# Low parts of weights by an accumulating DMA instead of a VectorE subtraction, in a two-layer hybrid decoder

## The chip, the cores and the metric

The kernel runs on one core of a Trainium2 chip. The time is device microseconds (us) of one execution of the whole program, from start to end; a run of the kernel before took 1132.09 us (median of three runs, 1131.34 to 1132.42). Engines are named as in the profile: PE is TensorE's matrix multiplication and PEld its weight load, DVE is VectorE, ACT is ScalarE, POOL is GpSimd, SP is SyncE, which issues the transfers. Transfers run on 16 DMA engines that all queues share.

## What is computed

Two decoder layers on 512 prompt tokens and 8 x 8 sample tokens (576 rows, D_MODEL 1024), all in float32:

```python
h = rmsnorm(x, g_norm)
z = h @ w_in                      # 1024 x 5700: rq rk rv rz aq ak av az iq ik iw gr ga
o_r, s_new = retention(rq, rk, rv, s0)
u_r = (group_norm(o_r) * silu(rz)) @ w_o_ret
o_a = sparse_attention(aq, ak, av, top-k by the indexer iq, iw, ik)
u_a = (o_a * silu(az)) @ w_o_att
x = x + (sigmoid(gr) * u_r + sigmoid(ga) * u_a) @ w_out
x = x + sigmoid(x @ w_ple_gate) * (p @ w_ple_proj)
```

Nearly all of the arithmetic is products of the 576 rows with weights. The outputs are the rows after two layers and the new keys, values and retention states.

## The kernel before, in words

**Two-part products.** A float32 factor is split into a high part, rounded to the type float32r (`fp32r` in the profile), and a low part, the factor minus its high part. A product is then three matmuls into one PSUM bank: high times high, high times low of the one factor, low times high of the other. In `proj_a` (lines 457 to 477) the weight is the stationary operand (`pm<-xh,whi`, `pm<-xl,whi`, `pm<-xh,wlo` in the profile, 288 columns each); in `proj_b` (479 to 497) and `proj_kx` (499 to 522) the rows are stationary and the weight moves (`pm<-whi,xh`, `pm<-whi,xl`, `pm<-wlo,xh`, 256 to 320 columns). In each, the low part of a weight is wanted first by the third matmul.

**Weights.** All weights of both layers are one sequence of 148 pieces, at most 128 x 1024 elements (512 KB); this text counts them from 0. `PLAN` sets the order. In layer 0: pieces 0 to 4 are kx (keys and values), 5 to 7 iq (the indexer's queries), 8 and 9 rv0, 10 and 11 rv1 (retention values), 12 to 15 az, 16 and 17 aq0, 18 and 19 aq1 (attention queries), then 12 pieces for retention heads, then gates and outputs: gr, ga, wo, wout, pp, wpg. Layer 1 repeats this from piece 74 (iq 79 to 81, rv0 82 and 83, rv1 84 and 85, aq1 92 and 93).

`load_weights` issues each load from SP into one of two staging buffers (`wst`, 128 x 1024). `convert` takes one of three buffers `whi` and one of three `wlo`, has ACT round the staged piece into `whi`, has DVE subtract into `wlo`, and then gives the staging buffer back. `drop`, or the end of `proj_b` and `proj_kx`, gives `whi` and `wlo` back when PE has used the piece. So at any time PE uses one or two pieces, and the rest of the three are ready or in preparation. In `proj_b` both pieces of a weight are used for each of five row tiles, so the second piece of the next weight finds a free buffer only at the end of the fifth tile.

**Side work.** Beside the projections run streams for the indexer's top-k, attention, retention and norms. Their matmuls stand between the projections' in PE's queue. Reciprocal square roots are one `pow` on POOL each, with DVE before and after it.

**Order.** `Streams` (from line 195) writes out each engine's instructions by list scheduling: of all streams' next instructions it takes the one that a model of the engines could start first. The engines then run their queues in that order and wait on semaphores. `_duration` and the DMA rule in `go` are that model's prices.

Of the kernel before, what the change touches and what calls it, by code (L numbers as in the profile page):

```python
# [11 lines left out]
FT = mybir.dt.float32  # L12
# [3 lines left out]
AF = mybir.ActivationFunctionType  # L16
OP = mybir.AluOpType
# [101 lines left out]
def _val(x):  # L119
    return x() if callable(x) else x  # L120
# [14 lines left out]
def _free(ap):  # L135
    n = 1
    for s, c in list(ap.ap)[1:]:
        n *= c
    return n


def _duration(eng, name, out, aps, a, k):
    n = max(_free(x) for x in aps)
    psum = any(x.space == PSUM for x in aps[1:])
    if eng == "PE":
        if name == "transpose":
            return 0.110
        lhs = aps[1]
        if lhs.dtype == FT:
            if _free(lhs) <= 32:  # L150
                return 0.030 + n * 0.4e-3
            return 4 * max(n, 64) / 2.4e3 * (0.55 if _free(lhs) <= 64 else 1.0)
        return max(n, 64) / 2.4e3 + 0.003
    if eng == "DVE":
        if name == "memset":
            return (n + 8) / 0.96e3
        ptr = sum(1 for x in aps[1:] if _free(x) == 1 and n > 4 and x.space != PSUM)
        if name in ("tensor_scalar", "tensor_copy") and not psum and all(x.dtype == FT for x in aps[:2]):
            return (n / 2 + 66) / 0.96e3 + 0.062 * min(ptr, 2)
        return (n + 64) / 0.96e3 + 0.062 * min(ptr, 2)  # L160
    if eng == "ACT":
        ptr = sum(1 for x in aps[1:] if _free(x) == 1 and n > 1)
        return (n + (61 if psum else 112)) / 1.2e3 + 0.093 * min(ptr, 2)
    if eng == "POOL":
        return 0.3 + 0.165 * n
    return {"page": 0.5, "gather": 0.74}.get(name, 0.47)

# [25 lines left out]


class Streams:
    """Emits the instructions of many sequential streams in the order in which a model of the engines could
    start them, so that each engine's program order follows what is ready."""

    HOP = {("DVE", "DVE"): 0.13, ("ACT", "ACT"): 0.13, ("POOL", "POOL"): 0.1, ("PE", "PE"): 0.0, ("SP", "SP"): 0.0,
           ("ACT", "PE"): 0.23, ("DVE", "PE"): 0.21, ("PE", "DVE"): 0.2, ("PE", "ACT"): 0.2, ("POOL", "DVE"): 0.07,  # L200
# [76 lines left out]
    def go(self):  # L277
        clock = self.clock
        while True:
            while self.run:  # L280
                st, value = self.run.pop(0)
                self._advance(st, value)
            if not self.heads:
                return
            best = None
            for i, st in enumerate(self.heads):
                key = (max(clock[st[3].eng], st[4]), st[1], st[2])
                if best is None or key < best[0]:
                    best = (key, i)
            st = self.heads.pop(best[1])  # L290
            op = st[3]
            start = best[0][0]
            op.fn(*op.a, **op.k)  # L293
            end = start + op.dur
            clock[op.eng] = end
            if op.eng == "SP" and op.name != "page":
                size = _val((op.a[0] if op.a else op.k["out"]).nbytes)
                self.dma = max(self.dma, start + 1.1) + size / 0.35e6
                end = self.dma + 1.0
            self._note(op, end)  # L300
            self._advance(st, None)
# [3 lines left out]
def tile_hybrid_decoder(ctx: ExitStack, tc: tile.TileContext, A, O):  # L305
    nc = tc.nc
    ctx.enter_context(tc.manual_schedule())
    K = Streams()
    V, S, PE, SP, G = (Engine(n, o) for n, o in (("DVE", nc.vector), ("ACT", nc.scalar), ("PE", nc.tensor),
                                                 ("SP", nc.sync), ("POOL", nc.gpsimd)))  # L310
# [7 lines left out]
    def slots(pool, name, shape, dtype, n):  # L318
        return Slots([pool.tile(shape, dtype, name=f"{name}{i}") for i in range(n)])
# [35 lines left out]
    WST = slots(cp, "wst", [128, 1024], FT, 2)  # L355
# [33 lines left out]
    ready, paged = Event(), Event()  # L389
    second, third = Event(), Event()  # L390

    # ---- weights: one ordered sequence of units, each split into two float32r parts as it lands
    W = {}

    class Unit:
# [32 lines left out]
    stage_ev = {}  # L428

    def load_weights(units):  # L430
        for n, (u, src, size) in enumerate(units):
            if n == 1:
                yield second
            if n == 3:
                K.set(third)
            t = yield Get(WST)
            yield SP.dma_start(t[:, :size], src)
            K.spawn(convert(u, t, size, stage_ev[n], stage_ev[n + 1]), PRIO["convert"])

    def convert(u, t, size, prev, done):  # L440
        yield prev
        hi = yield Get(WHI)
        lo = yield Get(WLO)
        yield S.activation(hi[:, :size], t[:, :size], AF.Copy)
        yield V.tensor_tensor(lo[:, :size], t[:, :size], hi[:, :size].bitcast(FT), OP.subtract)
        K.put(WST, t)
        K.set(u.evs[len(u.parts)])
        u.parts.append((hi, lo))
        K.set(u.ev)
        K.set(done)  # L450
# [106 lines left out]
    def layer(l, xh, xl, kxb):  # L557
# [3 lines left out]
        def side(gen, prio, *events):  # L561
            ev = Event()

            def wrap():
                yield from gen
                for e in events:
                    K.set(e)
                K.set(ev)

            sides.append(ev)  # L570
            K.spawn(wrap(), prio)
# [45 lines left out]
        def stats():  # L617
            yield V.memset(ssq[:, T:], 1.0)
            ps = yield Get(BANK["tr"])
            for j in range(5):  # L620
                yield PE.matmul(ps[:, j:j + 1], ssq[:, j * 128:(j + 1) * 128], ones, start=True, stop=True)
            yield from rsqrt(rcol[:, :5], ps[:, :5], 1.0 / D, EPS)
            K.put(BANK["tr"], ps)
            K.set(e_r)
            yield ready
            ps = yield Get(BANK["tr"])
            for j in range(4):
                yield PE.transpose(ps[:, j * 128:(j + 1) * 128], bc(rcol[:, j:j + 1], [128, 128]), ident)
            yield S.activation(R[:, :NP], ps, AF.Copy)
            K.put(BANK["tr"], ps)  # L630
            ps = yield Get(BANK["tr"])
            yield PE.transpose(ps[:, :128], bc(rcol[:, 4:5], [128, 128]), ident)
            yield S.activation(R[:, NP:], ps[:, :NS], AF.Copy)
            K.put(BANK["tr"], ps)
            K.set(e_rq)
# [262 lines left out]
        def head(j, u, g, kv, oT, done):  # L898
            L = max(256, (j + 1) * 128)
            bias = con("cb") if j == 0 else scs[j]  # L900
            q = qst[j, u][:, (g % 2) * 2 + kv]
            P = yield Get(T2)
            b = yield Get(BANK["tq"])
            ps = b[:, :L]
            yield PE.matmul(ps, q, kdh[:, 1 + kv, :L], start=True, stop=False)
            yield PE.matmul(ps, q, kdl[:, 1 + kv, :L], start=False, stop=True)
            yield from softmax(ps, bias, P[:, :L], b)
            PT = yield Get(T2)
            pT = yield Get(BANK["ta"])
            W_ = (j + 1) * 128  # L910
            for k in range(j + 1):
                yield PE.transpose(pT[:, k * 128:(k + 1) * 128], P[:, k * 128:(k + 1) * 128], ident)
            K.put(T2, P)
            yield S.activation(PT[:, :W_], pT[:, :W_], AF.Copy)
            K.put(BANK["ta"], pT)
            for k in range(j + 1):
                yield PE.matmul(oT[kv * 64:(kv + 1) * 64, g * 128:(g + 1) * 128], av[:, k, kv * 64:(kv + 1) * 64],
                                PT[:, k * 128:(k + 1) * 128], start=k == 0, stop=k == j)
            K.put(T2, PT)
            K.put(HD, None)  # L920
            K.set(done)

        HD = Slots([None] * HEADS_IN_FLIGHT)

        def attend():
            yield e_k
            for j in range(4):
# [4 lines left out]
                for u in range(2):  # L932
                    yield e_q[j, u]
                    for g in (2 * u, 2 * u + 1):
                        for kv in range(2):
                            yield Get(HD)
                            K.spawn(head(j, u, g, kv, oT, done), PRIO["attend"])
                yield done
# [256 lines left out]
        side(stats(), 0)  # L1195
        side(tables(), PRIO["tables"])
        for j in range(1, 4):
            side(indexer(j), PRIO["indexer"], e_sc[j])
        side(indexer_s(), PRIO["indexer_s"], e_sc[4])
        side(attend(), PRIO["attend"])  # L1200
        side(attend_s(), PRIO["attend_s"])
# [262 lines left out]

PLAN = _plan("kx iq rv0 rv1 az0 az1 az2 az3 aq0 aq1 rt0 rt1 rt2 rt3")
HEADS_IN_FLIGHT = 3
PRIO = dict(convert=0, load=1, tables=6, indexer=7, indexer_s=3, attend=3, attend_s=5, ret_p=6, ret_s=4)
NSLOT = dict(s4=3, qs=5, t2=5, hi=3, lo=3)

# [81 lines left out]
```

## Time and profile before

| | |
|---|---|
| runs | 1132.09 us median (1131.34 to 1132.42) |
| span of the profiled execution | 1130.3 us, 1.8 us under the median of the runs |
| instructions in the profile | 21562, of them 8586 on PE |
| share of the span in which each is busy | PE 99%, PEld 94%, DVE 64%, ACT 45%, POOL 4% |
| transfers | 105.92 MB, mean 94 GB/s; 93.61 MB read from HBM |
| granted TensorE clock | full in all 40 slices of the span |

The profile is one execution. Busy PE is modelled and says that matmuls follow each other without a gap that can be seen, not that each is at its shortest. What the transfers move by source: 96 loads of `in_wa`, 16 of `in_wb`, 16 of `in_wo` with 512 KB each are the bulk of the weights. No transfer is issued from POOL.

### The profile page before, as it was taken

The numbers are of one execution on the slowest core, as the hardware profiler recorded it, in microseconds if no ns is written. First come the engines' busy times: TensorE is split into PE (matmuls) and PEld (weight loads), VectorE is DVE, ScalarE is ACT, GpSimd is POOL, SyncE is SP. The second block draws the span as 40 slices with busy tenths as digits, with TensorE's granted clock in tenths as the row PEclk, the third lists the DMA queues.
The fourth block names the chain that finished last, engine by engine and source line by source line (L and its number), as shares of the span: only waits on it lengthen the run. The fifth ranks groups of instructions, "written<-read, shape, count | busy, mean of one in ns | idle before, by whom it ended". The sixth has DMA issues, their size and how long they took to land.

```text
span 1130.3 us, 21562 instructions
## 1 busy us (share of the span) xinstructions
PE 1116.5 (99%) x8586; PEld 1058.9 (94%) x8586; DVE 725.6 (64%) x1883; ACT 512.5 (45%) x1084; POOL 45.7 (4%) x52
## 2 busy tenths in 40 slices
PE   8999999999999999999999999999999999999998
PEld 7899988888899999999999999888889999999998
DVE  6799988876464444543658999888654553544343
ACT  6643566647443232324546336656563422222331
POOL 0100200000000000000010012000000000000000
PEclk9999999999999999999999999999999999999999
DMA  6442221322122222523336112222212222234231
GB/s 196 139 133 76 76 75 52 102 78 78 59 75 75 93 76 92 172 92 109 100 118 181 59 57 94 74 79 80 73 60 78 75 78 91 75 130 144 93 113 48
DMA packets 43895, 105.92 MB, mean 94 GB/s; under 512 B 6418, under 2 KB 18578, under 8 KB 43794
## 3 DMA queue, kind: packets, MB, share of 16 engines
q1 hardware_dynamic: 43794, 104.55, 27.4%
q8 instruction: 67, 1.10, 0.4%
q14 instruction: 34, 0.28, 0.1%
HBM read 93.61 MB, written 10.91 MB: 92 GB/s over the span
## 4 chain that ended last, share of the span: by engine, by line
PE 91%; DVE 4%; DMA 2%; ACT 2%; issue 1%; SPq 0%; POOL 0%; DVEq 0%; ACTq 0%; POOLq 0%
PE pm L293 72%; PE oT L293 5%; PE tq L293 4%; PE acc L293 3%; PE tr L293 3%; PE ta L293 3%; DVE wlo L293 1%; DMA wst<-in_wb 1%; ACT whi L293 1%; DVE misc L293 1%; DMA x<-in_xT 1%; DVE silz L293 0%; DMA wst<-in_wq 0%; DVE qs L293 0%; DVE ol L293 0%
## 5 line engine op out<-in xcount | busy, mean ns | idle before, releaser
L293 PE MATMUL pm<-xl,whi 128*128 128x288 f32 x1536 | 458.7, 299 | 0.0
L293 PE MATMUL pm<-xh,wlo 128*128 128x288 f32 x1536 | 458.4, 298 | 0.0
L293 PE MATMUL pm<-xh,whi 128*128 128x288 f32 x1536 | 458.0, 298 | 0.4 <-DVE misc L293 0.4
L293 PEld LDWEIGHTS pm<-xl,whi 128*128 128x128 f32 x1536 | 290.1, 189 | 3.2 <-issue 2.4
L293 PEld LDWEIGHTS pm<-xh,whi 128*128 128x128 f32 x1536 | 290.2, 189 | 2.9 <-issue 1.6
L293 PEld LDWEIGHTS pm<-xh,wlo 128*128 128x128 f32 x1536 | 289.9, 189 | 1.8 <-issue 1.4
L293 ACT ACTIVATE whi<-wst 128x1024 fp32r<-128x1024 f32 (+4 forms) x148 | 150.5, 1019 | 280.5 <-PE pm L293 207.7
L293 DVE TENSOR_TENSOR wlo<-wst,whi 128x1024 fp32r<-128x1024 f32 (+4 forms) x148 | 173.0, 1171 | 88.8 <-ACT whi L293 88.5
L293 PE MATMUL pm<-whi,xh 128*128 128x256 f32 (+2 forms) x416 | 117.2, 288 | 0.7 <-ACT xl L293 0.7
L293 PE MATMUL pm<-wlo,xh 128*128 128x256 f32 (+2 forms) x416 | 117.0, 289 | 0.0
L293 PE MATMUL pm<-whi,xl 128*128 128x256 f32 (+2 forms) x320 | 91.0, 284 | 0.0
L293 DVE TENSOR_TENSOR misc<-pm,R 128x288 f32<-128x288 f32 x64 | 29.2, 457 | 90.1 <-PE pm L293 88.7
L293 ACT ACTIVATE t2k<-t2k,sm 128x256 f32<-128x256 f32 (+3 forms) x136 | 75.6, 581 | 22.6 <-DVE sm L293 19.4
L293 PEld LDWEIGHTS pm<-whi,xh 128*128 128x128 f32 x416 | 78.7, 189 | 2.5 <-issue 1.2
L293 PEld LDWEIGHTS pm<-wlo,xh 128*128 128x128 f32 x416 | 78.7, 189 | 1.6 <-issue 1.1
L293 PE MATMUL pm<-oh,whi 128*128 128x288 f32 x240 | 71.0, 296 | 0.0
L293 PE MATMUL pm<-oh,wlo 128*128 128x288 f32 x240 | 70.9, 296 | 0.0
L293 PE MATMUL pm<-ol,whi 128*128 128x288 f32 x240 | 70.9, 295 | 0.0
L293 PEld LDWEIGHTS pm<-whi,xl 128*128 128x128 f32 x320 | 60.5, 189 | 0.1
L293 ACT ACTIVATE misc<-misc 128x288 f32<-128x288 f32 x64 | 27.9, 436 | 60.5 <-DVE misc L293 60.5
L293 DVE MAX8 sm<-xl 128x8 f32<-128x384 f32 (+2 forms) x96 | 52.3, 548 | 0.3
L293 DVE SCALAR_TENSOR_TENSOR misc<-misc,pm 128x288 f32<-128x288 f32 x60 | 26.8, 451 | 39.3 <-PE pm L293 39.3
(231 smaller groups left out, 1654.3 us busy)
## 6 DMA issues: line engine op xcount, KB each, us to landing
wst<-in_wa SPq DMA_DIRECT2D x96, 512.0 KB, 3.5
wst<-in_wb SPq DMA_DIRECT2D x16, 512.0 KB, 4.1
wst<-in_wo SPq DMA_DIRECT2D x16, 512.0 KB, 3.4
s<-in_ckv SPq DMA_DIRECT2D x32, 128.0 KB, 2.4
s<-in_s SPq DMA_DIRECT2D x8, 512.0 KB, 4.3
out_rss<-s SPq DMA_DIRECT2D x8, 512.0 KB, 2.6
x<-in_xT SPq DMA_DIRECT2D x8, 288.0 KB, 4.5
misc<-in_xT SPq DMA_DIRECT2D x8, 288.0 KB, 3.6
```

What stands on the lines that cost most here:

```text
L293: op.fn(*op.a, **op.k)
```

## The change

The first nine pieces (`DIRECT = 9`, kx, iq and the first of rv0, in layer 0) are split as before. For the other 139, ACT rounds the piece into `whi` and the staging buffer is given back at once; a second ACT instruction writes the negated high part into `wlo`; and POOL issues a DMA that reads the same weights from HBM once more and adds them to `wlo`. What stands in `wlo` is the same value as before. The list scheduler prices POOL's issue at 1.0 us and counts the transfer as it does those of SP.

```diff
@@ _duration
     if eng == "POOL":
+        if name == "dma_start":
+            return 1.0
         return 0.3 + 0.165 * n
@@ Streams.go
-            if op.eng == "SP" and op.name != "page":
+            if op.name in ("dma_start", "gather"):
                 size = _val((op.a[0] if op.a else op.k["out"]).nbytes)
                 self.dma = max(self.dma, start + 1.1) + size / 0.35e6
                 end = self.dma + 1.0
@@ load_weights
-            K.spawn(convert(u, t, size, stage_ev[n], stage_ev[n + 1]), PRIO["convert"])
+            K.spawn(convert(u, t, src, size, n, stage_ev[n], stage_ev[n + 1]), PRIO["convert"])
@@ convert
         yield S.activation(hi[:, :size], t[:, :size], AF.Copy)
-        yield V.tensor_tensor(lo[:, :size], t[:, :size], hi[:, :size].bitcast(FT), OP.subtract)
-        K.put(WST, t)
+        if n < DIRECT:
+            yield V.tensor_tensor(lo[:, :size], t[:, :size], hi[:, :size].bitcast(FT), OP.subtract)
+            K.put(WST, t)
+        else:
+            K.put(WST, t)
+            yield S.activation(lo[:, :size], hi[:, :size].bitcast(FT), AF.Copy, scale=-1.0)
+            yield Op("POOL", nc.gpsimd.dma_start, "dma_start", (lo[:, :size], src), {"accum_op": OP.add})
@@
+DIRECT = 9
```

On PE, at the start of aq1 in layer 0 (pieces 18 and 19; `whi_89` and `wlo_92` are piece 18, `whi_90` and `wlo_93` piece 19, `tq` the attention's logits, `ta` transposes), before:

```order
787 L293 MATMUL pm_70<-wlo_92,xh 128x256
788 L293 MATMUL pm_70<-whi_89,xh 128x256
789 L293 MATMUL pm_70<-whi_89,xl 128x256
790 L293 MATMUL pm_70<-wlo_92,xh 128x256
791 L293 MATMUL pm_70<-whi_90,xh 128x256
792 L293 MATMUL pm_70<-whi_90,xl 128x256
793 L293 MATMUL pm_70<-wlo_93,xh 128x256
```

and now:

```order
788 L295 MATMUL pm_70<-whi_89,xh 128x256
789 L295 MATMUL pm_70<-whi_89,xl 128x256
790 L295 MATMUL pm_70<-wlo_92,xh 128x256
791 L295 MATMUL pm_70<-whi_90,xh 128x256
792 L295 MATMUL pm_70<-whi_90,xl 128x256
793 L295 MATMUL tq_71<-kdh,qs_377 128x256
794 L295 MATMUL tq_71<-kdl,qs_377 128x256
795 L295 MATMUL ta_72<-cst,misc 128x128 x2
796 L295 MATMUL pm_70<-wlo_93,xh 128x256
```

Four short matmuls of the side work now stand ahead of the first use of piece 19's low part.

On ACT, while az is computed in layer 0 (`whi_91` and `wlo_94` are piece 17, `whi_89` and `wlo_92` piece 18, `tb` a temporary of the SiLU), before:

```order
109 L293 ACTIVATE whi_91<-wst_88 128x1024
110 L293 ACTIVATE tb_391<-silz_358 128x288
111 L293 ACTIVATE tb_390<-silz_358 128x288
112 L293 ACTIVATE t2k_386<-tq_71 128x512
113 L293 ACTIVATE t2k_384<-tq_71 128x512
114 L293 ACTIVATE whi_89<-wst_87 128x1024
115 L293 ACTIVATE tb_391<-silz_358 128x288
```

and now:

```order
120 L295 ACTIVATE whi_91<-wst_88 128x1024
121 L295 ACTIVATE tb_391<-silz_358 128x288
122 L295 ACTIVATE wlo_94<-whi_91 128x1024
123 L295 ACTIVATE tb_390<-silz_358 128x288
124 L295 ACTIVATE whi_89<-wst_87 128x1024
125 L295 ACTIVATE tb_391<-silz_358 128x288
126 L295 ACTIVATE wlo_92<-whi_89 128x1024
```

Each piece has a second ACT instruction of its full size, with one instruction of another stream between the two (so for 111 of the 139 pieces; two for 2, none for 26).

On POOL, from the end of kx to aq0 and aq1 in layer 0 (`sm` and `rsm` belong to the reciprocal square roots of the norms), before:

```order
12 L293 TENSOR_TENSOR sm_373<-rsm_98,mh 64x2
13 L293 TENSOR_TENSOR sm_369<-rsm_96,mh 128x4
14 L293 TENSOR_TENSOR sm_371<-rsm_97,mh 128x4
15 L293 TENSOR_TENSOR sm_373<-rsm_98,mh 128x4
16 L293 TENSOR_TENSOR sm_371<-rsm_96,mh 128x4
```

and now:

```order
20 L295 DMA wlo_93<-in_wb 128x1024
21 L295 DMA wlo_94<-in_wb 128x1024
22 L295 DMA wlo_92<-in_wb 128x1024
23 L295 TENSOR_TENSOR sm_372<-rsm_96,mh 128x4
24 L295 TENSOR_TENSOR sm_373<-rsm_97,mh 128x4
25 L295 TENSOR_TENSOR sm_369<-rsm_98,mh 128x4
26 L295 TENSOR_TENSOR sm_370<-rsm_96,mh 128x4
27 L295 DMA wlo_93<-in_wb 128x1024
28 L295 TENSOR_TENSOR sm_372<-rsm_97,mh 64x4
```

POOL's queue, which held the reciprocal square roots alone, now also holds 139 issues, each of which waits for its second ACT instruction.

## Rows read from the trace of the kernel before

**Rows 1.** Page, busy time: engine, us (share of the span), instructions.

```profile
PE 1116.5 (99%) x8586; PEld 1058.9 (94%) x8586; DVE 725.6 (64%) x1883; ACT 512.5 (45%) x1084; POOL 45.7 (4%) x52
```

**Rows 2.** Layer 0, two stretches: us; PE, PEld, DVE, ACT, POOL busy; clock; DMA.

```profile
113.00:325.00 212.00, 211.29 (x1678) 187.00 (x1677) 158.52 (x503) 123.22 (x300) 15.38 (x16) 1.00 0.21 74
325.00:553.00 228.00, 227.62 (x1717) 227.38 (x1716) 110.06 (x158) 78.00 (x123) 0.00 (x0) 1.00 0.29 99
```

**Rows 3.** Waits of PE: line and releaser, us in total, times, longest.

```profile
PE oT L293 <- ACT whi L293: 5.2, 1, 5.2
PE oT L293 <- DVE ol L293: 0.8, 2, 0.4
...
PE pm L293 <- DVE misc L293: 0.4, 2, 0.2
```

**Rows 4.** Chain of waits, shares of the span by engine.

```profile
PE 91%; DVE 4%; DMA 2%; ACT 2%; issue 1%; SPq 0%; POOL 0%; DVEq 0%; ACTq 0%; POOLq 0%
```

**Rows 5.** Groups of instructions, shapes apart: count, busy us, mean ns, idle before.

```profile
L293 ACT ACTIVATE whi<-wst 128x1024 fp32r<-128x1024 f32 x132 | 139.8, 1059 | 262.8 <-PE pm L293 195.9 <-issue 63.4 <-DMA wst<-in_wb 3.2
L293 DVE TENSOR_TENSOR wlo<-wst,whi 128x1024 fp32r<-128x1024 f32 x132 | 161.0, 1221 | 73.8 <-ACT whi L293 73.5
L293 ACT ACTIVATE misc<-pm 128x288 f32<-128x288 f32 x32 | 13.0, 406 | 37.8 <-PE pm L293 37.8
L293 POOL TENSOR_TENSOR sm<-rsm,mh 128x4 f32<-128x4 f32 (+3 forms) x30 | 29.5, 986 | 230.1 <-DVE rsm L293 223.9 <-DVE sm L293 6.1
```

**Rows 6.** Transfers: the queue's total; issues, KB each, median us to landing.

```profile
q1 hardware_dynamic: 43794, 104.55, 27.4%
...
wst<-in_wa SPq DMA_DIRECT2D x96, 512.0 KB, 3.5
...
wst<-in_wq SPq DMA_DIRECT2D x2, 260.0 KB, 3.1
```

**Rows 7.** Chain of waits in order of time, a load of rv1 in layer 1.

```profile
598.50 5.94 DMA wst<-in_wb
```

**Rows 8.** Timeline, piece 48: high part, subtraction, first use of the low part.

```profile
389.89 1.06 ACT L293 ACTIVATE whi<-wst 128x1024 fp32r<-128x1024 f32 x1 [4.98 <-PE pm L293]
391.19 1.22 DVE L293 TENSOR_TENSOR wlo<-wst,whi 128x1024 fp32r<-128x1024 f32 x1
402.82 0.30 PE L293 MATMUL pm<-oh,wlo 128*128 128x288 f32 x1
```

**Rows 9.** Timeline, pieces 9, 11, 19 and 82: high part, first use of the low part.

```profile
38.08 1.06 ACT L293 ACTIVATE whi<-wst 128x1024 fp32r<-128x1024 f32 x1
40.98 0.28 PE L293 MATMUL pm<-wlo,xh 128*128 128x256 f32 x1
...
56.09 1.06 ACT L293 ACTIVATE whi<-wst 128x1024 fp32r<-128x1024 f32 x1 [0.53 <-PE pm L293]
60.85 0.28 PE L293 MATMUL pm<-wlo,xh 128*128 128x256 f32 x1
...
116.03 1.06 ACT L293 ACTIVATE whi<-wst 128x1024 fp32r<-128x1024 f32 x1 [0.53 <-PE pm L293]
119.42 0.29 PE L293 MATMUL pm<-wlo,xh 128*128 128x256 f32 x1
...
595.40 1.06 ACT L293 ACTIVATE whi<-wst 128x1024 fp32r<-128x1024 f32 x1
597.78 0.38 PE L293 MATMUL pm<-wlo,xh 128*128 128x256 f32 x1
```

**Rows 10.** Timeline, pieces 13 and 81: high part, first use of the low part.

```profile
75.45 1.06 ACT L293 ACTIVATE whi<-wst 128x1024 fp32r<-128x1024 f32 x1
82.94 0.30 PE L293 MATMUL pm<-xh,wlo 128*128 128x288 f32 x1
...
584.60 0.64 ACT L293 ACTIVATE whi<-wst 128x520 fp32r<-128x520 f32 x1 [3.20 <-PE pm L293]
588.51 0.28 PE L293 MATMUL pm<-wlo,xh 128*128 128x260 f32 x1
```

More of the change, by code (lines that the diff above doesn't have):

```diff
@@ L437, in load_weights, with convert @@
             yield SP.dma_start(t[:, :size], src)
-            K.spawn(convert(u, t, size, stage_ev[n], stage_ev[n + 1]), PRIO["convert"])
-    def convert(u, t, size, prev, done):
+            K.spawn(convert(u, t, src, size, n, stage_ev[n], stage_ev[n + 1]), PRIO["convert"])
+    def convert(u, t, src, size, n, prev, done):
         yield prev
```

## The prediction

> **What bounds the kernel now.** I read the busy times first, then the stretches, the waits of PE, and last the timeline around single pieces of weights. PE is busy in 1116.5 of 1130.3 us, DVE in 725.6, ACT in 512.5, POOL in 45.7 [rows 1]. The stretches show that this is no average over unlike stages: in layer 0's attention PE is busy in 211.3 of 212 us, while DVE has 158.5 of work, and among the outputs PE is busy in 227.6 of 228 us with DVE at 110.1; the granted clock is 1.00 in both [rows 2]. PE's waits are small: one of 5.2 us at the very start, on ACT, and then parts of a microsecond, of which the largest that DVE ends are 0.8 and 0.4 us in total [rows 3]. The chain of waits is 91% PE and 4% DVE [rows 4]; 4% of 1130 is 45 us, but PE was running other matmuls beside most of that, as its busy time shows. So PE bounds the kernel, and what DVE gives up is worth a few us at most. The question is then only whether the low parts still come in time.
>
> **What is removed.** The change takes 139 subtractions off DVE, most of the 132 of full size at 1.22 us each, 161.0 us [rows 5]. In the stretches above DVE has room already, and the waits it ends make up about 2 us. I take the gain as nothing; were DVE's whole share of the chain to come back it would be 45 us, which is a rival below.
>
> **What is added, for one piece.** Before, a piece was ready 1.06 us (ACT) and 1.22 us (DVE) after its buffer came free, plus hops. Now four steps follow each other:
> - ACT rounds: 1.06 us [rows 5].
> - ACT writes the negated copy, of the same size and engine, so 1.06 us again. In most pieces one other ACT instruction stands between the two; a common one takes 0.41 us [rows 5].
> - Two hops between engines. The subtraction of piece 48 begins at 391.19, after the rounding that ends at 390.95, so 0.24 us at most [rows 8]; I take 0.2 in all.
> - POOL's issue and the transfer to its landing. No DMA from POOL and no accumulating one is in this trace, so this term, X, is bounded. From below: it moves the same 512 KB from the same tensor as the staging load, which takes 3.5 us from issue to landing [rows 6]; it can't be less than that, and no gain is possible from a step that was not there. From above: twice the slowest load of this size on the chain, 2 x 5.94 = 11.9 us [rows 7]. My value starts from 3.5. The queue moved 104.55 MB while holding 27.4% of 16 engines over 1130 us [rows 6], which is 310 us of all 16 and 2.96 us a MB, so 512 KB hold them for 1.55 us. The add needs `wlo` read as well: +1.55. The rounding that starts this chain also frees the staging buffer, so SP's next load shares the engines with the accumulation: +1.55. POOL must prepare the transfer; its nearest row is a small arithmetic operation of 0.99 us [rows 5]: +1.0. X = 7.6 us.
>
> So a piece is ready L = 1.06 + 0.41 + 1.06 + 0.2 + 7.6 = 10.3 us after its buffer came free (lowest, with X of 3.5: 6.2; highest, 14.6).
>
> The page "Collectives: The Full Stack" of the Trainium skill (The bandwidth ceiling) says that an add inside a DMA pushes two source reads through the read side and that this, not the adding, about halves the rate; that is the doubling assumed above, which no run here shows yet. The page "DMA: Bandwidth & Descriptors" (Anatomy of one DMA) fits 2.0 us plus bytes over 436 GB/s to a DMA from GpSimd; for 512 KB this gives 3.2 us, and the row of a load from SP says 3.5 [rows 6]. With the bytes doubled, an estimate by that page is 4.4 us for X, L would be 7.1, and the sum below some 23 instead of 49 us.
>
> **Which pieces can stand that.** The cover of a piece is the time from its rounding, which starts as its buffer comes free, to PE's first use of its low part. Among the outputs it is 402.82 - 389.89 = 12.9 us [rows 8]: PE has two other pieces to go through, each 48 matmuls of 228 / 1717 = 0.133 us, 6.4 us [rows 2]. That covers 10.3 us, with 2.6 to spare. In layer 0's attention pieces are used more slowly and the cover is longer. It is short where `proj_b` hands over: the second piece of the new weight gets its buffer only when the last row tile of the old one ends. Piece 9 (rv0) has 2.9 us, piece 11 (rv1) 4.8, piece 19 (aq1) 3.4, and piece 82 (rv0 in layer 1) 2.4 [rows 9]. Pieces 85 and 93 of layer 1 repeat 11 and 19. The scheduler moves little in front of these places: ahead of piece 19 four short matmuls, about half a us by 0.133 each, since it expects the transfer as cheap as one of SP's. PE's queue is in order, so nothing behind the third matmul can fill the hole. PE waits:
>
> - piece 9: 10.3 - 2.9 = 7.4
> - pieces 11 and 85: 10.3 - 4.8 = 5.5 each, 11.0
> - pieces 19 and 93: 10.3 - 3.4 = 6.9 each, 13.8
> - piece 82: 10.3 - 2.4 = 7.9
> - piece 13 (az), cover 7.5 [rows 10], and its like in layer 1: 2.8 each, 5.6
> - piece 81, the last of iq in layer 1, 128 x 520: cover 3.9 [rows 10]. Both ACT steps take 0.64, the load of half size takes 3.1 [rows 6], its two additions of 1.55 shrink to 0.79, so L = 0.64 + 0.41 + 0.64 + 0.2 + 3.1 + 0.79 + 0.79 + 1.0 = 7.6, and 3.7 are missing.
>
> Piece 83 follows 82 within 1.5 us and waits behind the same hole. Together 49.5 us. What hides the accumulations of the other pieces is PE's own queue; without that cover each would cost up to 10 us.
>
> **The rest.** ACT gets 139 more instructions, some 140 us, and stands at 512 of 1130; what queues behind them there are softmax and evacuations for PE. DVE ends fewer waits, ACT more: I set these against each other. On POOL reciprocal square roots stand behind issues that wait for ACT; DVE's norms wait for them, and behind those transposes. Each is written where the scheduler expects it to be ready, so I price it at nothing, at most the 1 us for which an issue holds POOL, a few times. SP's loads are issued a subtraction earlier, and none is late now. The extra 72 MB read from HBM hold the 16 engines for 139 x 2 x 1.55 = some 430 us beside 310, within the span.
>
> Sum: 1130.3 + 49.5 = 1179.8 in the profiled execution, whose span is 1.8 us under the median of the runs, so 1181.6, or 1182 us.
>
> **Rivals.**
> 1. The transfer outlasts even the long cover. The place is wo to wpg in both layers, the point X = 12.9 - 2.7 = 10.2 us. At X = 11.9 each piece is 1.7 us late, shared by two successive ones, 0.85 us on some 72 pieces (228 / 6.4 = 36 a layer) = 61 us; the tight places then cost 66 + 14 + 6 us; 1132 + 147 = 1279. For it: nothing here tells the rate of an accumulation. Against it: the engines are held 0.21 to 0.29 of the time [rows 2].
> 2. The holes also cost clock. The granted clock is 1.00 in both stretches [rows 2] with PE in work throughout, and no stretch at the lower level stands here to price it. If PE came back from each hole at half pace, for as long as the hole was, half of 49.5 would be lost again: 1182 + 25 = 1207. The page "TensorE: Matmul & The Clock Gate" of the Trainium skill (Part 1) says that the clock goes down from 2.4 to 1.2 GHz when TensorE idles; by that rule 1207 is the result, and the trace shows no drop so far, not even beside the 5.2 us at the start.
> 3. The transfer lands as a plain load does, X = 3.5: the tight pieces cost 3.3 + 2 x 1.4 + 2 x 2.8 + 3.8, piece 81 1.1, together 16.6; 1149.
> 4. Faster: DVE's relief in the attention of both layers (158.5 of 212 us busy there) lets PE's side matmuls start without waits, and all of the chain's 45 us come back, more than rival 3's 16.6: 1132 - 28 = 1104. It decides once the relief is worth more than the holes. For it: the 4% [rows 4]. Against it: PE's waits on DVE [rows 3].
>
> **How the numbers follow.** The forecast (X from 4.5 to 10) has 0.60, its own range 1155 to 1205; rival 1 0.12, rival 2 0.17, rival 3 0.07, rival 4 0.04. The range 1149 to 1245 leaves out rival 4 and most of rival 1, with the tail between. 0.2% is 2.3 us, about what a measurement of this kernel can tell from no change. Faster by more than that is rival 4, 0.04 with little to share; within it lies only the crossing between rivals 3 and 4, 0.03; the rest, 0.93, is slower.
>
> **What would show it.** In the new profile the waits of PE should name a DMA from POOL into `wlo` at some nine places, longest near the starts of rv0, rv1 and aq1, 5 to 8 us each, while wo to wpg show none and a period of 6.4 us. X can be read as POOL's median from issue to landing. If X is near 7.6 and PE has no such waits, the cover was misread. If wo to wpg are stretched, it is rival 1; a clock below 1.00 behind the holes, rival 2; shorter stretches of attention, rival 4.

## The result and the profile after

The changed kernel takes 1199.36 us (median of four runs, 1197.09 to 1200.67), the kernel before 1132.26 us on the same chip: a ratio of 1.0596, 95% interval 1.0583 to 1.0608, or 67 us more. The profiled execution has a span of 1196.7 us, 66.4 more than before. The forecast was 1182 us; its range, 1149 to 1245, holds the result, which is 17 us above the forecast.

First the page: busy time of each engine, the granted clock in 40 slices, the two queues, and the chain of waits.

```profile
PE 1135.9 (95%) x8586; PEld 1074.4 (90%) x8586; DVE 579.5 (48%) x1744; ACT 641.0 (54%) x1223; POOL 167.1 (14%) x191
...
PEclk9899899999999999999988898999999999999999
...
q0 software_dynamic: 20016, 71.07, 36.5%
q1 hardware_dynamic: 43794, 104.55, 26.5%
...
PE 80%; issue 7%; DMA 6%; DVE 3%; ACT 3%; POOL 1%; SPq 0%; POOLq 0%; DVEq 0%; ACTq 0%
```

DVE fell from 725.6 to 579.5 us and ACT rose from 512.5 to 641.0 [rows 1]; the chain is no longer 91% PE [rows 4]. PE stands still for 1196.7 - 1135.9 = 60.8 us, where it stood 13.8 before: 47.0 more. It is also busy 19.4 us longer with the same 8586 matmuls. The two make up the 66.4. Where they lie is told by PE's waits (us in total, times, longest):

```profile
PE pm L295 <- DMA wlo<-in_wb: 30.3, 8, 6.6
PE oT L295 <- ACT whi L295: 5.3, 1, 5.3
PE tq L295 <- DVE iqs L295: 2.9, 2, 2.0
PE tq L295 <- DVE sm L295: 2.6, 2, 2.3
PE oT L295 <- DMA wlo<-in_wk: 2.2, 2, 1.6
PE pm L295 <- DMA wlo<-in_wq: 2.1, 1, 2.1
PE oT L295 <- DVE ol L295: 2.1, 2, 1.1
PE ta L295 <- DVE qs L295: 1.8, 1, 1.8
```

The first line is new and the largest; no wait names a low part of `in_wa` or `in_wo`. The second is the start of the program, there before as well [rows 3]. Waits that name a transfer into `wlo` add up to 30.3 + 2.2 + 2.1 = 34.6 us, in eleven places. In the timeline of pieces 9, 82 and 85 (start, duration, engine; idle time and its releaser in brackets) the chain of one piece can be followed, as in [rows 9]:

```profile
38.35 1.06 ACT L295 ACTIVATE whi<-wst 128x1024 fp32r<-128x1024 f32 x1
40.13 1.04 ACT L295 ACTIVATE wlo<-whi 128x1024 fp32r<-128x1024 f32 x1
41.49 1.06 POOL L295 DMA_DIRECT2D wlo<-in_wb  x1 [5.25 <-ACT wlo L295]
43.55 0.39 PE L295 MATMUL tq<-kdh,iqs 128*128 128x256 f32 x1 [0.92 <-DVE iqs L295]
48.96 0.58 PE L295 MATMUL pm<-wlo,xh 128*128 128x256 f32 x1 [4.91 <-DMA wlo<-in_wb]
...
629.66 1.07 ACT L295 ACTIVATE whi<-wst 128x1024 fp32r<-128x1024 f32 x1
631.12 1.06 ACT L295 ACTIVATE wlo<-whi 128x1024 fp32r<-128x1024 f32 x1
632.48 0.92 POOL L295 DMA_DIRECT2D wlo<-in_wb  x1 [7.62 <-ACT wlo L295]
634.29 0.39 PE L295 MATMUL tq<-kdh,iqs 128*128 128x256 f32 x1 [1.98 <-DVE iqs L295]
640.83 0.58 PE L295 MATMUL pm<-wlo,xh 128*128 128x256 f32 x1 [6.04 <-DMA wlo<-in_wb]
...
664.66 1.05 ACT L295 ACTIVATE whi<-wst 128x1024 fp32r<-128x1024 f32 x1
666.02 1.05 ACT L295 ACTIVATE wlo<-whi 128x1024 fp32r<-128x1024 f32 x1
673.80 0.58 PE L295 MATMUL pm<-wlo,xh 128*128 128x256 f32 x1 [6.58 <-DMA wlo<-in_wb]
```

The low part is used 10.6, 11.2 and 9.1 us after the rounding began. At 43.55 and 634.29 stand side matmuls that the scheduler put ahead of the low part and that themselves wait for DVE: their idle time lies in the same hole. The matmul behind the hole takes 0.58 us, where it took 0.28 to 0.38 [rows 9]. The stretches show why; the first three lie in and behind the holes above, the last among the outputs, and the sum is over all seven stretches at the half clock (us; PE, PEld, DVE, ACT, POOL busy; clock; DMA share, GB/s):

```profile
44.78:55.02 10.24, 6.06 (x28) 6.06 (x29) 1.37 (x5) 3.42 (x7) 0.83 (x1) 0.50 0.81 241
635.28:645.52 10.24, 4.69 (x20) 4.35 (x21) 2.00 (x10) 4.16 (x9) 1.48 (x2) 0.50 0.98 239
669.41:679.65 10.24, 5.85 (x27) 5.85 (x28) 8.73 (x35) 0.76 (x3) 0.86 (x1) 0.50 0.73 149
...
340.00:580.00 240.00, 238.31 (x1792) 237.63 (x1792) 72.88 (x127) 117.70 (x169) 32.03 (x37) 1.00 0.80 179
...
sum 54.61, PE 34.65 PEld 33.67 DVE 26.29 ACT 17.96 POOL 8.33; mean PE 4.95 PEld 4.81 DVE 3.76 ACT 2.57 POOL 1.19
```

The granted clock is at the half level in seven stretches, each in or right behind a hole, 54.6 us together; PE is busy in 34.65 of them, so about 17.3 us of the 19.4 more busy time are the clock, if half the pace is lost there. (Matmuls of 256 columns begin 0.213 us apart in these stretches and 0.118 at the full clock; by that it would be 15.5.) Before, the clock was full wherever PE worked. Among the outputs next to nothing is lost, 1.7 us of 240 (0.4 of 228 before), though the DMA engines are busy there 0.80 of the time instead of 0.29 [rows 2].

### The profile page after: what moved, and what is told of

The parts are those of the page before. It is cut to its first block, busy times and chain, and to the rows that moved or that the text cites. A ratio compares the mean times of both kernels' runs of the same rounds, so it can differ in the third digit from the quotient of the medians.

```text
span 1196.7 us, 21825 instructions
## 1 busy us (share of the span) xinstructions
PE 1135.9 (95%) x8586; PEld 1074.4 (90%) x8586; DVE 579.5 (48%) x1744; ACT 641.0 (54%) x1223; POOL 167.1 (14%) x191
## 3 DMA queue, kind: packets, MB, share of 16 engines
q0 software_dynamic: 20016, 71.07, 36.5%
## 4 chain that ended last, share of the span: by engine, by line
PE 80%; issue 7%; DMA 6%; DVE 3%; ACT 3%; POOL 1%; SPq 0%; POOLq 0%; DVEq 0%; ACTq 0%
PE pm L295 64%; DMA wlo<-in_wb 5%; PE oT L295 4%; PE tq L295 3%; PE acc L295 3%; PE tr L295 3%; PE ta L295 3%; ACT wlo L295 1%; DVE misc L295 1%; POOL wlo L295 1%; DVE xl L295 1%; DMA wlo<-in_wq 1%; ACT whi L295 1%; ACT xh L295 0%; DVE rot L295 0%
## 5 line engine op out<-in xcount | busy, mean ns | idle before, releaser
L295 POOL DMA_DIRECT2D wlo<-in_wa x96 | 84.0, 875 | 547.3 <-ACT wlo L295 495.7
L295 PE MATMUL pm<-wlo,xh 128*128 128x256 f32 (+2 forms) x416 | 124.8, 307 | 32.5 <-DMA wlo<-in_wb 30.3
L295 ACT ACTIVATE wlo<-whi 128x1024 fp32r<-128x1024 f32 (+3 forms) x139 | 143.0, 1029 | 2.3 <-issue 1.4
L295 PE MATMUL pm<-whi,xh 128*128 128x256 f32 (+2 forms) x416 | 123.0, 302 | 0.7 <-ACT xl L295 0.7
L295 PEld LDWEIGHTS pm<-wlo,xh 128*128 128x128 f32 x416 | 85.6, 206 | 36.9 <-DMA wlo<-in_wb 32.3
L295 PE MATMUL pm<-whi,xl 128*128 128x256 f32 (+2 forms) x320 | 96.2, 301 | 0.0
L295 PEld LDWEIGHTS pm<-whi,xh 128*128 128x128 f32 x416 | 85.8, 206 | 1.2 <-ACT xl L295 0.9
L295 PEld LDWEIGHTS pm<-whi,xl 128*128 128x128 f32 x320 | 66.0, 206 | 0.3 <-issue 0.2
L295 ACT ACTIVATE t2k<-ta 128x256 f32<-128x256 f32 (+3 forms) x80 | 32.4, 413 | 38.5 <-PE ta L295 37.9
```

## Experiments

**Which pieces.** The first two runs split the change by pieces: 23 come several to a weight (kx, iq, rv, aq), 116 alone.

```diff
-        if n < DIRECT:
+        if n < DIRECT or len(u.srcs) == 1:    # e2: DVE for the single pieces
+        if n < DIRECT or len(u.srcs) > 1:     # e1: DVE for the others
```

> The converse: only the 23 pieces of kx, iq, rv and aq from the tenth piece on are formed by the accumulating DMA, the 116 single ones by DVE. Theory A: nearly all of the loss stays, 1185 to 1199 us, with the same long waits at rv0, rv1 and aq1 and the half clock behind them. Rival B: 1132 + 67 x 23 / 139 = 1143 us.

Measured: 1198.75 us, ratio 1.0588 (1.0570 to 1.0606). The 23 pieces alone cost all of it, with the same wait:

```profile
PE pm L295 <- DMA wlo<-in_wb: 34.8, 8, 6.6
```

> The pieces of weights that come several to a unit (kx, iq, rv, aq; 23 of the 139 changed ones) are split by DVE again; the 116 single ones keep the accumulating DMA. Theory A (PE waits only where the cover is short, and loses clock behind those waits): both go, 1130 to 1137 us, granted clock 1.00 in all slices, no wait of PE on a DMA into wlo over 1 us. Rival B (what costs is spread over all accumulations: the doubled reads, ACT's second pass, POOL's queue, 67 us over 139 of them): 116 remain, 1132 + 67 x 116 / 139 = 1188 us. Rival C (DVE's relief was worth something and hidden under the waits): below 1128 us.

Measured: 1151.63 us, ratio 1.0183 (1.0169 to 1.0197): neither theory. The halves cost 67 and 20 us and together 67, so they don't add up. The waits and two places in the timeline say what the 20 are:

```profile
PE pm L295 <- DMA wlo<-in_wa: 5.4, 2, 2.8
PE ta L295 <- ACT t2k L295: 3.5, 2, 1.7
PE oT L295 <- ACT t2k L295: 2.1, 3, 1.0
```

```profile
75.54 1.06 ACT L295 ACTIVATE whi<-wst 128x1024 fp32r<-128x1024 f32 x1 [0.20 <-PE pm L295]
...
86.02 0.61 PE L295 MATMUL pm<-xh,wlo 128*128 128x288 f32 x1 [2.83 <-DMA wlo<-in_wa]
...
138.53 1.04 ACT L295 ACTIVATE wlo<-whi 128x1024 fp32r<-128x1024 f32 x1
139.60 0.28 ACT L295 ACTIVATE t2k<-ta 128x128 f32<-128x128 f32 x1
...
139.93 0.33 PE L295 MATMUL ta<-cst,misc 64*128 64x64 f32 x2 [1.74 <-ACT t2k L295]
```

Piece 13 is rounded at 75.54 and its low part is used at 86.02, 10.5 us later: it waits the 2.8 us that the prediction had for it, and piece 87 2.6. In the changed kernel the same piece is rounded at 91.13 and used at 99.98, 8.8 us later, without a wait: POOL's transfer took 6.1 us there and 7.7 here, and PE, behind its other holes, came 1.3 us later. And at 139.60 a small ACT instruction, for which PE waits, stands behind the negation that ends at 139.57: ACT's second pass is not free. PE's idle time is 14.3 us over before's; 10.25 us at the half clock make some 5 more. The two runs also differ from the changed kernel in order, since the scheduler wrote a new one for each.

**What X is made of.** POOL's transfer as a plain copy:

```diff
-            ... (lo[:, :size], src), {"accum_op": OP.add})
+            ... (lo[:, :size], src), {})
```

> The changed kernel with POOL's transfer as a plain copy instead of an addition; wlo then holds the weight itself and not its low part, the rest is the same. It tells what of X (POOL's issue to landing, 6.2 us in the median with the addition) is the addition. Theory A (the addition reads a second operand): X falls to 3.5 (a load from SP) + 1.0 (POOL) = 4.5 us in the median, the waits at some nine places shrink by about 1.7 us each, 1177 to 1187 us. Rival B (POOL's path and the shared engines set X, the addition is free): X stays at 5.8 to 6.4 and the time at 1195 to 1201.

Measured: 1184.67 us, ratio 1.0461 (1.0442 to 1.0479). POOL's transfers (first the changed kernel, then the copy):

```profile
DMA to landing us min/median/max: 3.7/6.2/9.6
```

```profile
q0 software_dynamic: 20016, 71.07, 21.2%
...
DMA to landing us min/median/max: 3.0/4.7/7.9
```

Theory A. The addition is 1.5 us of X, and 1.5 us less save 14.7 us of time: 9.8 us for each us of X, not far from the eleven places that wait. The order on PE is that of the changed kernel.

**Cover.** Four `whi` and `wlo` buffers; the first try gave up an s4 buffer for the space, the second a t2k, a tb and an so buffer (all are tiles of the side work).

```diff
-NSLOT = dict(s4=3, qs=5, t2=5, hi=3, lo=3)
+NSLOT = dict(s4=2, qs=5, t2=5, hi=4, lo=4)    # e5
+NSLOT = dict(s4=3, qs=5, t2=4, hi=4, lo=4)    # e5b, with one tb and one so
```

> The changed kernel with four whi and four wlo buffers in place of three each; for the space one of three s4 buffers of the attention is given up. All 139 accumulations stay, as do the second pass on ACT and the second read. Theory A (cover): the second piece of a weight in proj_b gets its buffer a whole weight earlier, over 10 us of cover everywhere, and waits and half clock go: 1132 to 1142 us. Rival B (the accumulations load ACT, POOL or the DMA engines): 1190 us and more, with PE's waits moved, not gone. If the lost s4 buffer hurts the attention, PE's waits on ACT or DVE in the attention show it, up to 10 us.

Measured: 1191.87 us, ratio 1.0534 (1.0518 to 1.0550). Only two waits on `wlo<-in_wb` are left, 5.2 us, but the end of each attention became late: between 300 and 360 us PE is busy in 47.38 of 60, with new waits on ACT, DVE and a load of `s`. The try changed two things; the next one keeps s4.

> Four whi and four wlo buffers again, with all three s4 buffers kept; the space comes from one t2k, one tb and one so buffer. In the first try the waits at rv1, aq0 and aq1 were gone, those at the first rv piece of each layer (2.9 and 3.0 us at the low part, with side work late before it) stayed, and the end of each layer's attention lost some 25 us. Theory A (cover is the cause, the 25 us were the s4 buffer): 1132 + two places of about 9 us with their half clock + ACT's later side work, about 5 = 1150 to 1160 us. Rival B (accumulations late in the attention cost the 25 us): again 1185 and more. If tb, so or t2k are missed, waits of PE on ACT t2k or DVE in the attention tell of it.

Measured: 1156.49 us, ratio 1.0218 (1.0201 to 1.0235), as theory A has it. 137 of 139 low parts come in time, all accumulations kept; two places remain:

```profile
PE pm L295 <- DMA wlo<-in_wb: 7.2, 2, 3.7
PE oT L295 <- ACT whi L295: 5.6, 2, 5.2
PE ta L295 <- DVE kdl L295: 2.6, 1, 2.6
```

**Where the cover is long, and ACT.** Accumulation for the 84 output pieces alone; then ACT's second pass alone, into a tile that nobody reads; then the negation with DVE adding.

```diff
+        if n < DIRECT or n % 74 < 32:         # e9: DVE up to the retention heads
```

> DVE for the first 32 pieces of each layer (kx to the retention heads), the accumulating DMA only for the 84 pieces of gr, ga, wo, wout, pp and wpg, whose cover is 12.9 us in the profile before and whose low parts come 8.5 us after the rounding in the median. Theory A (an accumulation with enough cover is free): 1132 to 1135 us, granted clock 1.00, at most 1.2 us of waits on ACT at pp. Rival B (the 20 us that the 116 single pieces cost in the kernel with the multi-piece units by DVE are spread over them): 1132 + 20 x 84 / 116 = 1146 us. Rival C (DVE's relief is worth something): below 1129.

Measured: 1137.67 us, ratio 1.0051 (1.0034 to 1.0067), 2.7 us above theory A's range. The granted clock is full while PE works, no wait names a transfer, and the span is 4.9 us longer; the profile names 2.1 us of waits on DVE's `ol` (0.8 before) and 1.2 on ACT's `pp` (none before). By the waits the transfers cost nothing there, what stands behind ACT a little. DVE, relieved by 96 us, gave nothing back that can be seen.

```diff
+        if n >= DIRECT:                       # e10, behind DVE's subtraction
+            yield S.activation(spare[:, :size], hi[:, :size].bitcast(FT), AF.Copy, scale=-1.0)
```

> The kernel before's way of splitting (DVE subtracts) for all pieces, and beside it, for the 139 pieces, ACT writes the negated high part into a spare tile that nobody reads. It has ACT's 143 us of added work alone: no longer chain, no DMA from POOL, DVE not relieved. Theory A (ACT's added work costs a few us where evacuations and softmax stand behind it): 1134 to 1142 us. Rival B (as the prediction priced it): within 0.2% of before, 1130 to 1134. Rival C (the 33 us of the kernel with the addition on DVE were ACT's load in the attention): over 1150.

Measured: 1140.12 us, ratio 1.0072 (1.0057 to 1.0088): theory A by its number. ACT's added work costs 8.4 us without any transfer. It is not ACT alone, though: a piece counts as ready only behind the added instruction, so the scheduler wrote another order, on PE from its 249th matmul on. PE's longest new wait names DVE, and behind it 3.4 us of work run at the half clock:

```profile
PE pm L295 <- DVE misc L295: 2.5, 1, 2.5
```

```diff
-            K.put(WST, t)
             yield S.activation(lo[:, :size], hi[:, :size].bitcast(FT), AF.Copy, scale=-1.0)
-            yield Op("POOL", nc.gpsimd.dma_start, ...)
+            yield V.tensor_tensor(lo[:, :size], t[:, :size], lo[:, :size].bitcast(FT), OP.add)
+            K.put(WST, t)
```

> No DMA from POOL: ACT rounds, ACT writes the negated high part, DVE adds the staged weights to it, and then the staging buffer is given back. It leaves ACT's second pass and takes X away. L = 1.06 + 0.41 + 1.06 + 0.2 + 1.22 = 4.0 us, covers at the tight places 2.4 to 4.8: waits of 1.6 (piece 82), 1.1 (9), 0.6 (19, 93), together 4 us. Theory A (ACT's second pass is not quite free: in the kernel with the multi-piece units by DVE, PE waited 1.7 and 0.9 us a layer for ACT's t2k behind a negation): 1132 + 4 + 5 = 1141, 1137 to 1146 us. Rival B (ACT is free, as the prediction had it): 1134 to 1137. Rival C (ACT's second pass is the main cost, X a minor one): over 1165.

Measured: 1165.52 us, ratio 1.0290 (1.0272 to 1.0307), rival C by its number. Its waits at the low parts are as computed (4.5 us on DVE's `wlo`), but at the end of layer 0's attention others stand:

```profile
PE tr L295 <- ACT xh L295: 3.8, 1, 3.8
PE acc L295 <- ACT xh L295: 2.2, 1, 2.2
```

Of the 33 us some 9 are the half clock, at which 17.9 us of PE's work run. ACT's load alone does not make this (e10); DVE's full load, ACT's, a later staging buffer and a new order come together here, and which of them does it was not tried.

**The clock.** Matmuls of a zero tile fill the holes and add nothing to the sum; the order is otherwise the same.

```diff
+                    if i == 2 and j == tiles[0] and k % per == 0:
+                        for _ in range(u.fill.get(k // per, 0)):
+                            f = PE.matmul(ps[:, :n], x, zero[:, :n], start=False, stop=False)
```

> The changed kernel with 274 added matmuls of a zero tile (128 x 256, they add nothing to the sum), 12 to 55 of them directly ahead of the matmul that waits at nine places (rv0, rv1, aq0 and aq1 in layer 0; iq, rv0, rv1, aq0 and aq1 in layer 1), by 0.117 us each a little shorter than the hole there. The order on every engine is otherwise the same. Theory A (idle PE costs clock): the granted clock stays 1.00; in the profile of the changed kernel 34.7 us of PE's work ran at the half level, half of which comes back, 1199 - 17 = 1182 us (1177 to 1187). Rival D (the whole 54.6 us at the half level are lost in half): 1199 - 27 = 1172. Rival E (the clock falls for another reason, or the lost pace is hidden behind the next wait): 1199 within 3 us.

Measured: 1196.91 us, ratio 1.0574 (1.0558 to 1.0590). The clock's mean is 0.995 (0.976 before the filling), 10.0 us of PE's work are left at the half level, and the time is hardly less. One filling stood at piece 81, where there is no hole, so it was run again.

> The filled kernel again, with the zero matmuls where the trace of the first try shows the holes: none at the last iq piece of layer 1 (18 stood there without a hole and took 2.1 us), 17 at the iq piece before it, 60 at the first rv piece of layer 1, the others by one to seven changed. Order otherwise that of the changed kernel. Theory A (half of PE's 34.7 us at the half level come back): granted clock 1.00, 1181 to 1187 us. Theory E (where the transfers are late for their own reasons, a faster PE only waits longer; in the first try the low parts at 82 and 85 took 1.2 and 2.7 us longer): only layer 0's share and some of layer 1's come back, 1189 to 1196. Rival F (the clock is worth nothing): 1199 within 2.

Measured: 1193.07 us (five runs, 1188.64 to 1196.28), ratio 1.0533 (1.0514 to 1.0552), which does not overlap the changed kernel's: in theory E's range, some 7 us of the 17 come back. The profiled run is the slowest of the five, 1196.28, and in it 16.7 us of PE's work are still at the half level, in five stretches, where it was 34.65. The first place shows where some of the rest goes. The stretch behind piece 9's hole now has the full clock and 88 matmuls, 35 of them the filling; what was begun at 54.68 us is begun at 50.91. Then PE waits at a place where it did not wait before, the clock falls behind that wait, where it was full in the changed kernel, and by 68 us the lead is 0.2 us:

```profile
44.78:55.02 10.24, 10.24 (x88) 10.04 (x86) 3.78 (x12) 5.21 (x12) 0.88 (x1) 1.00 0.84 240
...
65.64:69.06 3.42, 3.42 (x18) 3.04 (x21) 2.49 (x9) 1.69 (x4) 0.00 (x0) 0.50 0.10 36
```

```profile
64.71 0.75 PE L296 MATMUL acc<-t2k,cst 128*64 128x320 f32 x2 [2.44 <-DVE t2k L296]
```

The filling also cost time itself. At piece 82 it overshot by 1.4 us, the clock having fallen inside it: the low part landed at 642.57 us and its matmul began at 644.01. At seven of the nine places together such matmuls began 4.9 us behind the landings. So 7 us came back here, but what a full clock without overshoot would give back is not shown.

**The scheduler's price.** 

```diff
-                end = self.dma + 1.0
+                end = self.dma + (4.5 if op.eng == "POOL" else 1.0)
```

> The changed kernel with one number changed in the scheduler's model: a DMA from POOL ends 4.5 us after its bytes, not 1.0. It moves side matmuls into the holes: 13 in place of 4 at piece 9 and 20 in place of 5 at the first rv piece of layer 1, hardly any elsewhere. Theory A (the holes are lost only as far as nothing fills them): 24 more matmuls of 0.1 to 0.2 us, 3 to 5 us, and up to as much again of clock: 1189 to 1197 us. Rival B (what is moved in front waits for DVE or ACT itself): 1197 to 1202.

Measured: 1210.40 us, ratio 1.0686 (1.0670 to 1.0702), slower than either theory. The wait on `wlo<-in_wb` halves, but what was moved in front waits too:

```profile
PE pm L295 <- DMA wlo<-in_wb: 15.9, 4, 6.7
PE ta L295 <- DVE qs L295: 8.8, 5, 2.9
...
PE tq L295 <- ACT t2k L295: 4.4, 3, 2.9
PE pm L295 <- DMA wlo<-in_wa: 3.2, 2, 2.9
```

**Cover everywhere.** The kernel of e5b with the two pieces left there by DVE.

```diff
+        if n < DIRECT or n in (9, 83):
```

> Four whi and four wlo buffers with all s4 buffers kept, as in the run of 1156 us, and the two pieces whose low part was still late there, the second of rv0 in each layer (9 and 83), by DVE: 137 accumulations remain. Theory A (late low parts were all but ACT's load): the two places with their half clock go, some 16 to 18 us; what is left is ACT's second pass, 8.4 us when it stood alone: 1138 to 1144 us, no wait of PE on a DMA into wlo over 0.5 us, granted clock 1.00. Rival B (137 accumulations cost something beside that, in the engines or on POOL): 1147 and more. Rival C (with DVE relieved, ACT's pass costs nothing): 1131 to 1135.

Measured: 1147.41 us (1143.24 to 1150.28), ratio 1.0145 (1.0123 to 1.0166). The low parts are in time, the clock in the profiled run is 1.00 throughout:

```profile
PE acc L295 <- DVE t2k L295: 2.5, 1, 2.5
...
PE pm L295 <- DMA wlo<-in_wb: 0.4, 1, 0.4
```

Of 15.6 us over before 8.4 are what ACT's pass cost in e10. The median lies at the edge of B. The profiled run is the fastest of the four, 1143.24 us or 11.4 over before, and the only one with the full clock: the others have a mean of 0.993 to 0.998. So part of the other 7 is clock that some runs lose; whether the rest is the t2k, tb and so buffers given up, the order or the accumulations' own is open. No version beat the kernel before.

## Why the prediction was right, step by step

The range held the result, and the waits came close to the forecast. Its middle was 17 us low because two terms stood at nothing, the clock and ACT; and what happened is rival 2 in kind, the same waits with the clock on top, 1207.

- **PE bounds, and DVE's relief is worth nothing**: right. 146 us off DVE made nothing faster. Rival 4 wanted 45 us back from the attention; e11, with DVE relieved there as in the changed kernel and the low parts in time, is still 15.6 us slower than before; 45 us back do not show. (e9 relieves DVE among the outputs only.)
- **One piece, L = 10.3 us**: 10.6, 11.2 and 9.1 at pieces 9, 82 and 85. X was 6.2 us in the median, 7.1 at the `in_wb` pieces, for 7.6. Its second operand is 1.5 in the median (forecast 1.55, e4); POOL's preparation and the sharing are 4.7 - 3.5 = 1.2, for 2.55. That 7.1 lies so near 7.6 is in part luck: the forecast began from the 3.5 us of an `in_wa` load, while rv and aq come from `in_wb`, whose loads took longer before the change:

```profile
wst<-in_wb SPq DMA_DIRECT2D x16, 512.0 KB, 4.1
```

At the `in_wb` pieces the addition is 7.1 - 5.1 = 2.0 (e4's median there is 5.1) and the rest 5.1 - 4.1 = 1.0. In engine time, 36.5% of 1196.7 us for 71.07 MB is 6.1 us a MB (437 us in all, for 430 forecast), 1.7 times the 3.5 of the plain copy from the same queue (e4) and twice the 3.0 of SP's queue. In time to landing the addition cost a third, 6.2 for 4.7. The page "Collectives: The Full Stack" of the Trainium skill (The bandwidth ceiling) says that two source reads about halve the rate; the engine time agrees roughly, the time to landing does not.

- **The waits, 49.5 us**: 43.8, in idle us at each place, with that of side matmuls in the same hole (34.6 name a transfer, 9.2 name DVE or ACT, behind which the low part was not there yet either):

| piece | forecast | measured |
|---|---|---|
| 9 | 7.4 | 0.8 + 0.9 + 4.9 = 6.6 |
| 11, 85 | 5.5 each | 4.5, 6.6 |
| 19, 93 | 6.9 each | 5.6, 5.3 |
| 82 | 7.9 | 2.0 + 6.0 = 8.0 |
| 13, 87 | 2.8 each | none (2.8 and 2.6 in e1) |
| 81 | 3.7 | none; 2.1 at piece 80 before it |
| 17, 91 | none | 1.4, 1.5 |
| kx, layer 1 | none | 2.2 |

Pieces 13 and 87 came in time, 13 by a later PE and a shorter X, as the comparison with e1 shows; 17 and 91, the second pieces of aq0, I had not listed. The last iq piece of layer 1 was in time, the one before it not. At the six places that came as listed it is 36.6 for 40.1; the 9.3 us of 13, 87 and 81 did not come, and 7.2 came where none was listed. That the two totals lie so close is in part luck as well.

- **Outputs, cover 12.9**: right. Piece 48 is rounded at 413.65 and its low part used at 426.58, 12.9 us later, and e9 shows 84 such pieces with no wait on a transfer.
- **The clock, nothing**: the step that failed by size. The central sum had no term for it; 15.5 to 17.3 us of it are in the profile. Rival 2 was the same waits with this term added, and its sign, a clock below 1.00 behind the holes, is there; the 1199 measured lie nearer to its 1207 than to 1182. The page "TensorE: Matmul & The Clock Gate" of the Trainium skill (Part 1) says that the clock falls when TensorE idles. This trace agrees at seven places, though not in the 5.3 us at the start, where the clock was full. The lost pace need not be the price: with half of the work or more restored to the full clock, e3 and e3b gained 2.5 and 7 us, as PE met other waits, lost clock elsewhere and was held by the filling; the shares are not separated.
- **ACT at nothing**: wrong by some 8 us where the pass stands without the transfers, its new order included (e10). In the changed kernel the profile names only small waits of this kind beside the holes; how much the holes hide was not measured there.

So 1130.3 + 43.8 + 17.3 leaves 5.3 us of the span 1196.7: 3.2 of idle time at other places (1.3 more on DVE's `ol` and 1.3 on ACT's `pp` among them) and 2.1 of busy time.

## What to carry to other kernels

Before a step that ends in time is lengthened, list the cover of every one of its uses, not the mean: 23 pieces with short covers, at which PE waited in eleven places, cost all 67 us here, and 84 with long ones 5.6. The costs of its two halves need not add up (67 and 20 us, together 67): each hole moves what comes after it. An engine at half load still has something queued behind a new pass; adding that pass alone shows the price, together with that of the order which the scheduler then writes.

## What the runs showed of the hardware beyond this

- The same 139 transfers from POOL held the engines 36.5% of 1196.7 us with the addition and 21.2% of 1182.6 without, 6.1 against 3.5 us a MB; POOL itself was busy 167.1 us against 120.3, a third of a microsecond more for each issue.
- A hole cost PE more than its length: in the changed kernel the half clock stayed granted for stretches of 3.4 to 10.2 us that reached past the hole, with PE at work again in 34.65 of 54.6 us.
- Filling the holes cut PE's work at the half level from 34.65 us to 10.0 (e3) and 16.7 (e3b's profiled run). The spans of these two runs are 1.4 and 2.2 us shorter, where half of the work restored would be 12.3 and 9.0. Part of the difference is the filling's overshoot (4.9 us in e3b), part of it are waits that stood next.
